# A two-layer hybrid trunk on one core: another pool order, split transposes and a TensorE sum at the start

## The chip, the cores and the metric

The kernel runs on one NeuronCore of one Trainium2 chip. The metric is device time of one execution in microseconds. Three runs of the kernel before gave 1827.31, 1830.92 and 1836.54 us, so the median is 1830.92 us.

## The reference

One step of a two-layer trunk on 640 tokens of width 1024 (512 latent tokens, 128 context tokens), all in float32:

- adaLN modulation: `m = silu(cond) @ w_mod + b_mod`, one vector of 6 x 1024 for each of the two conditions and each layer, `w_mod` being 1024 x 6144 in each layer;
- sub-layer 1: `h = rms(x) * (1 + scale) + shift`, one input projection `h @ w_in`, and three head groups beside each other: a diagonal complex state-space scan in both directions, latent attention with eight heads, and chunked gMLP. Then a norm for each group, one output projection and a gated residual;
- sub-layer 2: the second modulated norm, a gated feed-forward layer with a depthwise convolution of width 3 (`d_ff` 2816), and a gated residual.

For the scan each state needs `a_bar = exp(A * dt)` with `dt = exp(log_dt)`, its powers, and `(a_bar - 1) / A`. These come from `ssm_a_re`, `ssm_a_im` and `ssm_log_dt`. The initial states `state_ssm_re` and `state_ssm_im` enter only where a scan starts.

## The kernel before, in words

Activations are held transposed: `xT` is 128 partitions x 8 x 642, the eight slices (`k`) being the eight blocks of 128 features, with the latent tokens in columns 0 to 511 and the context tokens in 514 to 641. Each product of the large projections is three matmuls on split operands (`mm3`, lines 141 to 143): weights are loaded into a `raw` buffer, ScalarE rounds them to `whi` (L117) and VectorE makes the remainder `wlo` (L118). Token columns are done in two halves.

A planner orders the instructions: it takes them by the order of the program, simulates when their operands and buffers are ready, and writes one fixed stream for each engine. Within its stream an engine executes strictly in order. DMAs are issued from the streams of SP (SPq), ScalarE (ACTq) and GpSimd (POOL), so an issue that waits holds what stands behind it. A buffer can be overwritten only when all its readers are done, and pools that are opened after another was closed on the same side take the same addresses, so that they wait for the former users.

The start of the program, in the order of `run`:

- `consts`, `cond`: the identity matrix, and SiLU of the two conditioning vectors as `sT`.
- `ssm_scalars`: five 64x64 tables (real and imaginary part of A, `log_dt`, two states) are loaded on ACTq (L455, L450), transposed by TensorE into one PSUM bank `ssc`, and copied as one piece into `stab` (L460, L461). From there VectorE alone computes `dt`, sine, cosine, exponentials and powers (`exp_parts`, `sincos`, `complex_mul`; L384 to L436 and L470 to L522). Its last operations write `pw`, `rho`, `sf` and `r8`.
- `params(0)`: rows of small parameters are loaded from GpSimd's queue into a pool `prm0` on the right side, transposed by TensorE (`pa<-rows`), and copied by VectorE into `prm` and `cw` (L189, L198). The pool is closed.
- `load_x`: five tiles of 128 tokens (four `x_sample`, one `x_prompt`) are loaded by SPq into the three `raw` buffers of the pool `wp`, transposed by TensorE (`xin`), and copied to `xT` by ScalarE (L289).
- A pool `pre` on the right side, with eight `raw` buffers for `w_mod`: its addresses are those of `prm0`. `mod_blocks` loads four blocks of 512 columns, each in four loads of 512 KB (L257), multiplies them by `sT` (L261), copies the result (L267, `modev`), transposes it (`modt`) and reduces it (L240 to L247) to the columns of `mod`.
- `begin_layer`: the sum of squares of `xT` for the first half (`norm_stats`), the reciprocal root (`rsqrt`), the broadcast (`bcast`, `nbc`) and the modulated norm (`norm_apply`: `nt` L353, `hh` L357, `hl` L358). The second half follows at the head of `mixers` through `norm`. `norm_stats` squares the eight slices on ScalarE into `nsq` (L331); VectorE adds them to `nacc` (L332); TensorE sums over the partitions with a column of ones (L341, `nst`).

Then `mixers` starts. The pool `ssm` lies on the right side where `pre` lay, and its first use is a memset of `uT` on GpSimd (L870). GpSimd then computes the scan's rotation tables (`Tr`) and the tables of one of the four groups of channels (`q = 3`), while VectorE makes those of `q = 0, 1, 2` (`bb`, `G`, `Q`; `ssm_tables`), with transposes on TensorE (`we`). The tables go to DRAM and are loaded again for the scans (L690 to L696). The pool with `hh` and `hl` lies on the left side where the pool of `ssm_scalars` lay (memsets L1665).

Of the kernel before, what the change touches and what calls it, by code (L numbers as in the profile page):

```python
# [10 lines left out]
F32 = mybir.dt.float32  # L11
F32R = mybir.dt.float32r
I32 = mybir.dt.int32
AF = mybir.ActivationFunctionType
OP = mybir.AluOpType
# [5 lines left out]
KT = 8  # L21
# [13 lines left out]
def bc(ap, shape):  # L35
    return ap.to_broadcast(list(shape))
# [11 lines left out]
class Trunk:  # L48
# [260 lines left out]

    def norm(self, pool, l, which, lo, hi, hh, hl):  # L310

        r = self.norm_stats(pool, lo, hi)

        def rest():
            pb = self.pz("nbc")
            self.bcast(pool, *r, pb)
            self.norm_apply(pool, l, which, lo, hi, hh, hl, pb)

        return rest

    def norm_stats(self, pool, lo, hi):

        nc = self.nc
        n = hi - lo
        acc = pool.tile([128, 322], F32, name=self.uid("nacc"), tag="nacc", bufs=2)
        for k in range(KT):
            if k == 0:
                nc.scalar.activation(acc[:, :n], self.xT[:, k, lo:hi], AF.Square)
            else:
                sq = pool.tile([128, 322], F32, name=self.uid("nsq"), tag="nsq", bufs=2)  # L330
                nc.scalar.activation(sq[:, :n], self.xT[:, k, lo:hi], AF.Square)  # L331
                nc.vector.tensor_tensor(acc[:, :n], acc[:, :n], sq[:, :n], op=OP.add)  # L332
        blocks = []
        for a, b, _ in spans(lo, hi):
            blocks += list(range(a, b - 127, 128))
            if (b - a) % 128:
                blocks.append(b - 128)
        nb = len(blocks)
        ps = self.pz("nst")
        for i, b in enumerate(blocks):  # L340
            nc.tensor.matmul(ps[:, i:i + 1], acc[:, b - lo:b - lo + 128], self.ones[:, 0:1],  # L341
                             start=True, stop=True)
        v = self.smt([128, nb], f"nv{nb}")
        nc.vector.tensor_scalar(v, ps[:, :nb], 1.0 / D, EPS, op0=OP.mult, op1=OP.add)
        return self.rsqrt(v, nb), [b - lo for b in blocks]
# [93 lines left out]
    def ssm_scalars(self):  # L439


        nc, cp, I, V = self.nc, self.cp, self.I, self.nc.vector
        with self.tc.tile_pool(name="ssc", bufs=1) as pool:
            ps = self.pa("ssc")
            for i, nm in enumerate(("ssm_a_re", "ssm_a_im", "ssm_log_dt",
                                    "state_ssm_re", "state_ssm_im")):
                rows = pool.tile([64, 64], F32, name=self.uid("srow"), tag="srow", bufs=5)
                if nm == "ssm_log_dt":
                    col = pool.tile([64, 1], F32, name="sdt")
                    nc.scalar.dma_start(  # L450
                        out=col, in_=I[nm].rearrange("l d (g o) -> (l d g) o", o=1))
                    V.tensor_copy(rows, bc(col, [64, 64]))
                else:
                    src = I[nm] if nm[1] == "s" else I[nm][0]
                    nc.scalar.dma_start(out=rows, in_=src.rearrange("l d g p -> (l d g) p"))  # L455
                self.tr(ps[:64, i * 64:(i + 1) * 64], rows, 64)
            tab = pool.tile([128, 5, 32], F32, name="stab")
            pv = ps[:64, :320].rearrange("p (a h g) -> p a h g", a=20, h=2)
            tv = tab.rearrange("p i (a g) -> p (i a) g", g=8)
            V.tensor_copy(tv[0:64], pv[:, :, 0, :])  # L460
            V.tensor_copy(tv[64:128], pv[:, :, 1, :])  # L461
            are, aim = tab[:, 0, :], tab[:, 1, :]
            self.h0 = cp.tile([128, 2, 32], F32, name="h0")
            V.tensor_copy(self.h0, tab[:, 3:5, :])

            def t(s, sh=(128, 32)):
                return pool.tile(list(sh), F32, name=self.uid(s), tag=s)

            ldt = t("ldt")
            V.tensor_copy(ldt, tab[:, 2, :])  # L470
            dt, _ = self.exp_parts(pool, ldt, 32)
            ax = t("ax")
            V.tensor_tensor(ax, are, dt, op=OP.mult)
            th = t("th", (128, 8, 32))
            V.tensor_tensor(th[:, 0], aim, dt, op=OP.mult)
            for j in range(1, 8):
                V.tensor_scalar(th[:, j], th[:, 0], float(1 << (j + 2)), None, op0=OP.mult)
            ea, em = self.exp_parts(pool, ax, 32)
            sn, cm = self.sincos(pool, th.rearrange("p a b -> p (a b)"), 256)
            snv = sn.rearrange("p (a b) -> p a b", a=8)  # L480
            cmv = cm.rearrange("p (a b) -> p a b", a=8)
            self.rho = cp.tile([128, 7, 2, 32], F32, name="rho")
            V.tensor_scalar(self.rho[:, :, 0, :], cmv[:, 1:8], 1.0, None, op0=OP.add)
            V.tensor_copy(self.rho[:, :, 1, :], snv[:, 1:8])
            self.pw = cp.tile([128, 9, 3, 32], F32, name="pw")
            pw = self.pw
            V.memset(pw[:, 0, 0, :], 1.0)
            V.memset(pw[:, 0, 1, :], 0.0)
            x = t("x")
            V.tensor_tensor(x, ea, cmv[:, 0], op=OP.mult)  # L490
            V.tensor_tensor(pw[:, 1, 0, :], x, ea, op=OP.add)
            V.tensor_tensor(pw[:, 1, 1, :], ea, snv[:, 0], op=OP.mult)
            nre = t("nre")
            V.tensor_tensor(nre, x, em, op=OP.add)
            nim = pw[:, 1, 1, :]
            den, d2 = t("den"), t("d2")
            V.tensor_tensor(den, are, are, op=OP.mult)
            V.tensor_tensor(d2, aim, aim, op=OP.mult)
            V.tensor_tensor(den, den, d2, op=OP.add)
            V.reciprocal(den, den)  # L500
            self.f = cp.tile([128, 2, 32], F32, name="sf")
            y1, y2 = t("y1"), t("y2")
            V.tensor_tensor(y1, nre, are, op=OP.mult)
            V.tensor_tensor(y2, nim, aim, op=OP.mult)
            V.tensor_tensor(y1, y1, y2, op=OP.add)
            V.tensor_tensor(self.f[:, 0], y1, den, op=OP.mult)
            V.tensor_tensor(y1, nim, are, op=OP.mult)
            V.tensor_tensor(y2, nre, aim, op=OP.mult)
            V.tensor_tensor(y1, y1, y2, op=OP.subtract)
            V.tensor_tensor(self.f[:, 1], y1, den, op=OP.mult)  # L510
            for k in (1, 2, 4):
                sh = [128, k, 32]
                tm = [t(f"cm{i}{k}", sh) for i in range(2)]
                b_re = bc(pw[:, k:k + 1, 0, :], sh)
                b_im = bc(pw[:, k:k + 1, 1, :], sh)
                self.complex_mul(V, pw[:, k + 1:2 * k + 1, 0, :], pw[:, k + 1:2 * k + 1, 1, :],
                                 pw[:, 1:k + 1, 0, :], pw[:, 1:k + 1, 1, :], b_re, b_im, tm)
            V.tensor_scalar(pw[:, :, 2, :], pw[:, :, 1, :], -1.0, None, op0=OP.mult)
            self.r8 = cp.tile([128, 32], F32, name="r8")
            V.tensor_tensor(self.r8, ea, ea, op=OP.mult)  # L520
            V.tensor_tensor(self.r8, self.r8, self.r8, op=OP.mult)
            V.tensor_tensor(self.r8, self.r8, self.r8, op=OP.mult)  # L522
        self.WEd, self.Qd, self.Td, self.Wd = (
            [[self.dp.tile(sh, F32, name=f"{nm}{l}{q}") for q in range(4)] for l in range(DEPTH)]
            for nm, sh in (("WEd", [128, 2, 2, 2, 128]), ("Qd", [128, 2, 2, 2, 128]),
                           ("Td", [128, 2, 2, 2, NS]), ("Wd", [8, 16, 4, 128])))
        self.Ud = [self.dp.tile([256, 8, NC], F32, name=f"Ud{l}") for l in range(DEPTH)]
        self.Yd = [self.dp.tile([16, 128, NC], F32, name=f"Yd{l}") for l in range(DEPTH)]
# [1077 lines left out]
    def run(self):  # L1606
        nc, tc = self.nc, self.tc
        with self.banks(True):
            self.consts()
            self.cond()  # L1610
            self.ssm_scalars()
            self.params(0)
            self.load_x()
            self.late_consts()
            with tc.tile_pool(name="pre", bufs=1, side="right") as pre:
                mix = self.begin_layer(0, self.mod_blocks(0, (2, 0, 3, 1), pre))
        for l in range(DEPTH):
            sa, sb = self.sides
# [49 lines left out]
    def begin_layer(self, l, modulate=None):  # L1668
# [7 lines left out]
        if modulate:  # L1676
            for _ in range(8):
                next(modulate)
            r = self.norm_stats(N, 0, 320)
            for _ in range(2):  # L1680
                next(modulate, None)
            pb = self.pb("nbc")[:, 0]
# [73 lines left out]
```

## Time and profile before

| what | value |
|---|---|
| median of three runs | 1830.92 us (1827.31 to 1836.54) |
| the profiled execution | 1831.83 us, span 1830.0 us |
| PE busy | 1708.6 us, 93% of the span |
| PEld busy | 1499.7 us, 82% |
| DVE busy | 1158.5 us, 63% |
| ACT busy | 681.7 us, 37% |
| POOL busy | 311.4 us, 17% |
| DMA, mean | 100 GB/s, 182.44 MB |
| chain that ended last | PE 75%, DVE 10%, DMA 8%, ACT 4% |

The span runs from the first to the last instruction; the profiled execution's own time is 1.8 us longer than it. Busy shares are means over the whole span: the first 300 us and the rest have different limits, and the table does not tell them apart. The rows further below do.

### The profile page before, as it was taken

The page shows a single profiled execution, that of the slowest core. Times are in us where ns is not written, and L with a number is a line of the kernel's source. Part 1 is how long each engine was busy: PE and PEld are TensorE (multiplying, and loading weights), DVE is VectorE, ACT ScalarE, POOL GpSimd, SP SyncE. Part 2 cuts the span into 40 slices and gives each one's busy share as a digit, 9 for nine tenths or more (in the row PEclk, how much of TensorE's full clock was granted, in tenths as well). Part 3 has the DMA queues.
Part 4 walks back from the last instruction along what each step waited for, and adds up shares of the span by engine and source line. Part 5 has one row for each costly group of instructions (what it writes and reads, how often), then busy time and mean ns, then how long its engine had stood idle before and what let it go on. Part 6 is the DMA issues. An engine that isn't in the chain of part 4 may idle for free.

```text
span 1830.0 us, 28203 instructions
## 1 busy us (share of the span) xinstructions
PE 1708.6 (93%) x10864; PEld 1499.7 (82%) x10864; DVE 1158.5 (63%) x2421; ACT 681.7 (37%) x1210; POOL 311.4 (17%) x738
## 2 busy tenths in 40 slices
PE   6869789998999999999999888999989999999998
PEld 2668644478889999999999785445989999999998
DVE  6887875667664546456566668475786464555554
ACT  4334444433442424224244355353344232332241
POOL 2886200000195060540000210000000000000000
PEclk8989799999999999999999888999989999999999
DMA  9265453301453523223122633430222131221221
GB/s 297 70 177 152 113 166 122 105 24 47 129 160 111 152 55 117 76 81 110 47 78 79 169 87 121 157 127 1 70 70 93 35 104 47 92 89 39 81 82 58
DMA packets 192998, 182.44 MB, mean 100 GB/s; under 512 B 33438, under 2 KB 153052, under 8 KB 192864
## 3 DMA queue, kind: packets, MB, share of 16 engines
q1 hardware_dynamic: 170160, 154.33, 27.5%
q0 software_dynamic: 8272, 23.87, 4.4%
q10 hardware_dynamic: 14432, 2.44, 0.7%
q8 instruction: 86, 1.41, 0.3%
q14 instruction: 48, 0.39, 0.1%
HBM read 161.94 MB, written 18.64 MB: 99 GB/s over the span
## 4 chain that ended last, share of the span: by engine, by line
PE 75%; DVE 10%; DMA 8%; ACT 4%; issue 2%; POOL 1%; ACTq 1%; DVEq 0%; POOLq 0%
PE up L141 11%; PE up L143 11%; PE up L142 10%; PE dn L142 5%; PE dn L143 5%; PE dn L141 5%; PE mod L261 3%; DMA raw<-w_mod 3%; PE o L1287 3%; PE wo L141 1%; PE wo L143 1%; PE wo L142 1%; DVE wlo L118 1%; DMA raw<-ffn_w_up 1%; PE s L1267 1%
## 5 line engine op out<-in xcount | busy, mean ns | idle before, releaser
L141 PE MATMUL up<-hh,whi 128*128 128x322 f32 x1408 | 436.8, 315 | 9.8 <-ACT hh L357 8.9
L142 PE MATMUL up<-hl,whi 128*128 128x322 f32 x1408 | 439.2, 313 | 1.8 <-DVE hl L358 1.8
L143 PE MATMUL up<-hh,wlo 128*128 128x322 f32 x1408 | 439.8, 314 | 0.0
L141 PEld LDWEIGHTS up<-hh,whi 128*128 128x128 f32 x1408 | 266.1, 190 | 21.8 <-issue 10.8
L142 PEld LDWEIGHTS up<-hl,whi 128*128 128x128 f32 x1408 | 268.3, 191 | 2.7 <-DVE hl L358 2.7
L143 PEld LDWEIGHTS up<-hh,wlo 128*128 128x128 f32 x1408 | 267.3, 190 | 1.0 <-issue 1.0
L118 DVE TENSOR_TENSOR wlo<-raw,whi 128x1024 fp32r<-128x1024 f32 (+1 forms) x116 | 147.4, 1272 | 155.2 <-ACT whi L117 146.5
L142 PE MATMUL dn<-glo,dh 128*128 128x322 f32 (+1 forms) x704 | 217.7, 311 | 0.0
L143 PE MATMUL dn<-gh,dl 128*128 128x322 f32 (+1 forms) x704 | 217.4, 310 | 0.0
L141 PE MATMUL dn<-gh,dh 128*128 128x322 f32 (+1 forms) x704 | 208.9, 310 | 2.3 <-DVE xT L1501 1.5
L1501 DVE SCALAR_TENSOR_TENSOR xT<-dn,mod,xT 128x320 f32<-128x320 f32 (+2 forms) x288 | 112.1, 435 | 128.2 <-PE dn L143 128.1
L117 ACT CAST whi<-raw 128x1024 fp32r<-128x1024 f32 (+1 forms) x116 | 120.6, 1041 | 157.1 <-PE up L142 63.8
L1532 ACT ACTIVATE cv<-up,prm,cw 128x321 f32<-128x321 f32 x88 | 54.1, 619 | 259.0 <-PE up L143 255.0
L143 PEld LDWEIGHTS dn<-gh,dl 128*128 128x128 f32 x704 | 132.9, 189 | 0.0
L141 PEld LDWEIGHTS dn<-gh,dh 128*128 128x128 f32 x704 | 130.4, 189 | 2.8 <-DVE xT L1501 1.8
L142 PEld LDWEIGHTS dn<-glo,dh 128*128 128x128 f32 x704 | 132.7, 188 | 0.0
L261 PE MATMUL mod<-raw,sT 128*32 128x512 f32 x384 | 89.7, 642 | 21.7 <-DMA raw<-w_mod 19.8
L1533 DVE SCALAR_TENSOR_TENSOR cv<-up,cw,cv 128x320 f32<-128x320 f32 x88 | 48.3, 549 | 74.3 <-ACT cv L1532 74.1
L118 DVE TENSOR_TENSOR dl<-raw,dh 128x1024 fp32r<-128x1024 f32 x44 | 53.9, 1224 | 38.3 <-ACT dh L117 38.2
L1250 DVE TENSOR_REDUCE nml<-mx 128x1 f32<-128x640 f32 x64 | 51.1, 819 | 28.3 <-PE mx L1248 28.2
L117 ACT CAST dh<-raw 128x1024 fp32r<-128x1024 f32 x44 | 46.1, 1048 | 50.7 <-DMA raw<-ffn_w_down 44.5
L141 PE MATMUL wo<-yh,whi 128*128 128x322 f32 (+1 forms) x192 | 60.0, 318 | 1.7 <-ACT yh L117 0.9
(472 smaller groups left out, 3367.4 us busy)
## 6 DMA issues: line engine op xcount, KB each, us to landing
raw<-w_mod SPq DMA_DIRECT2D x96, 512.0 KB, 4.3
raw<-ffn_w_up SPq DMA_DIRECT2D x88, 512.0 KB, 3.9
raw<-ffn_w_down SPq DMA_DIRECT2D x44, 512.0 KB, 3.4
raw<-w_in SPq DMA_DIRECT2D x10, 512.0 KB, 5.0
we<-WEd POOLq DMA_DIRECT2D x8, 512.0 KB, 4.4
qt<-Qd POOLq DMA_DIRECT2D x8, 512.0 KB, 5.0
raw<-w_out SPq DMA_DIRECT2D x16, 256.0 KB, 4.8
raw<-w_out SPq DMA_DIRECT2D x8, 512.0 KB, 3.4
```

What stands on the lines that cost most here:

```text
L117: self.nc.scalar.copy(hi, raw)
L118: self.nc.vector.tensor_tensor(lo, raw, hi.bitcast(F32), op=OP.subtract)
L141: mm(ps, wh, xh, start=start, stop=False)
L142: mm(ps, wh, xl, start=False, stop=False)
L143: mm(ps, wl, xh, start=False, stop=stop)
L261: nc.tensor.matmul(ps[c:c + 32, :], self.sT[:, k, :], rv[:, j, :], start=k < 4, stop=k >= 4)
L1250: V.tensor_reduce(nm[:, tt:tt + 1], pb[:, :, :320], axis=AX.XY, op=OP.max, negate=True)
L1267: mm(ps, kh[i][:, kc_], qh[i], start=True, stop=False)
L1287: mm(pb[i * 64:(i + 1) * 64, 0], Vt[:, kt, 2 * p + i], Ps[i][kt], start=kt == 0, stop=kt == 4)
L1501: self.nc.vector.scalar_tensor_tensor(self.xT[:, m, a:b], po[:, a - lo:b - lo], self.modcol(l, gi, m, c), self.xT[:, m, a:b], op0=OP.mult, ...
L1532: A.activation(z[:, 0:321], po[:, 0:321], AF.Identity, bias=b, scale=c1)
L1533: V.scalar_tensor_tensor(z[:, 1:321], po[:, 0:320], c0, z[:, 1:321], op0=OP.mult, op1=OP.add)
```

## The change

Four edits, all of which act ahead of the first matmul on the modulated activations of layer 0:

1. The pool `pre` is opened ahead of `cond`, `ssm_scalars`, `params(0)` and `load_x`, so that its addresses are no longer those of `prm0`.
2. `ssm_scalars` transposes `log_dt` and the two parts of A first, into one bank, and copies them to `stab`. The two states are transposed into another bank at the end of the function and copied straight to `h0`.
3. `norm_stats` gets an argument. Where it is 0 (the first norm of layer 0, both halves) no `nacc` is made: TensorE multiplies each `nsq` by the column of ones and accumulates over the eight slices in one bank.
4. That bank comes from the pool `PA` (two banks at this stage) and not from `PS`.

```diff
-        r = self.norm_stats(pool, lo, hi)
+        r = self.norm_stats(pool, lo, hi, l + which)
...
-    def norm_stats(self, pool, lo, hi):
+    def norm_stats(self, pool, lo, hi, l=1):
...
+        ps = None if l else self.pa("nst")
+        acc = pool.tile([128, 322], F32, name=self.uid("nacc"), tag="nacc", bufs=2) if l else None
+        for k in range(KT):
+            if k == 0 and l:
+                nc.scalar.activation(acc[:, :n], self.xT[:, k, lo:hi], AF.Square)
+                continue
+            sq = pool.tile([128, 322], F32, name=self.uid("nsq"), tag="nsq", bufs=2)
+            nc.scalar.activation(sq[:, :n], self.xT[:, k, lo:hi], AF.Square)
+            if l:
+                nc.vector.tensor_tensor(acc[:, :n], acc[:, :n], sq[:, :n], op=OP.add)
+                continue
+            for i, b in enumerate(blocks):
+                nc.tensor.matmul(ps[:, i:i + 1], sq[:, b - lo:b - lo + 128], self.ones[:, 0:1],
+                                 start=k == 0 and i == 0, stop=k == KT - 1 and i == nb - 1)
...
+            tab = pool.tile([128, 3, 32], F32, name="stab")
+            rows_of(("ssm_log_dt", "ssm_a_re", "ssm_a_im"), tab)
...
+            self.h0 = cp.tile([128, 2, 32], F32, name="h0")
+            rows_of(("state_ssm_re", "state_ssm_im"), self.h0)
...
-            self.cond()
-            self.ssm_scalars()
-            self.params(0)
-            self.load_x()
-            self.late_consts()
             with tc.tile_pool(name="pre", bufs=1, side="right") as pre:
+                self.cond()
+                self.ssm_scalars()
+                self.params(0)
+                self.load_x()
+                self.late_consts()
                 mix = self.begin_layer(0, self.mod_blocks(0, (2, 0, 3, 1), pre))
...
-            r = self.norm_stats(N, 0, 320)
+            r = self.norm_stats(N, 0, 320, l)
```

`rows_of(names, tile)` is the former loop of loads and transposes over the given names, followed by the two copies of the bank to the two halves of the partitions of `tile`.

## Rows read from the trace of the kernel before

**Rows 1.** The page: busy tenths of the span in 40 equal slices.
```profile
PE   6869789998999999999999888999989999999998
...
POOL 2886200000195060540000210000000000000000
```

**Rows 2.** Windows to 55 us: busy us and count of each engine, clock, DMA share, GB/s.
```profile
0.00:10.00 10.00, 3.92 (x16) 3.02 (x17) 0.43 (x4) 2.48 (x3) 7.21 (x20) 1.00 0.68 195
10.00:20.00 10.00, 7.30 (x35) 6.16 (x33) 4.38 (x26) 4.73 (x7) 4.45 (x13) 1.00 0.91 247
20.00:35.00 15.00, 9.69 (x32) 1.67 (x32) 13.51 (x52) 8.60 (x18) 0.00 (x0) 0.66 1.01 341
35.00:50.00 15.00, 11.17 (x46) 3.11 (x46) 14.49 (x81) 3.08 (x5) 0.00 (x0) 0.89 1.00 354
50.00:55.00 5.00, 2.35 (x14) 1.33 (x15) 5.00 (x25) 2.02 (x6) 1.96 (x14) 1.00 0.16 41
```

**Rows 3.** Timeline of GpSimd: start us, us, what, idle before and its releaser.
```profile
50.75 0.12 POOL L1665 MEMSET hh<- 128x16 f32 x1 [35.26 <-issue]
...
53.16 0.13 POOL L870 MEMSET uT<- 128x16 f32 x1 [2.23 <-PE mod L261]
...
151.63 0.61 POOL L690 DMA_DIRECT2D we<-WEd  x1
```

**Rows 4.** Windows from 53 us to the scans' first load.
```profile
53.00:70.00 17.00, 15.09 (x97) 14.43 (x96) 12.84 (x37) 7.39 (x18) 16.79 (x62) 0.90 0.10 11
70.00:110.00 40.00, 32.97 (x229) 28.91 (x228) 37.06 (x88) 16.60 (x47) 38.20 (x104) 0.96 0.45 118
110.00:151.60 41.60, 30.86 (x264) 26.28 (x265) 33.59 (x75) 15.03 (x41) 32.73 (x71) 0.79 0.67 183
```

**Rows 5.** Timeline of VectorE: the scan constants' first copy, the parameter copy, the last powers.
```profile
11.89 0.32 DVE L460 COPY stab<-ssc 64x160 f32<-64x160 f32 x1 [5.39 <-PE ssc L147]
...
19.01 0.27 DVE L189 COPY prm<-pa 128x109 f32<-128x109 f32 x1 [3.45 <-PE pa L147]
...
51.33 0.31 DVE L518 TENSOR_SCALAR pw<-pw 128x288 f32<-128x288 f32 x1
```

**Rows 6.** Timeline of TensorE: transposes of tables, x tiles and parameters, and the last modulation matmuls.
```profile
6.55 0.31 PE L147 MATMUL ssc<-ident,srow 64*64 64x64 f32 x1 [1.97 <-DVE srow L452]
...
15.32 3.56 PE L147 MATMUL xin<-ident,raw 128*128 128x128 f32 x16 [1.57 <-DMA raw<-x_sample]
18.72 0.38 PE L147 MATMUL pa<-ident,rows 109*128 109x109 f32 x3
...
52.03 1.05 PE L261 MATMUL mod<-raw,sT 128*32 128x512 f32 x4
```

**Rows 7.** Timeline of SP's DMA issues to 55 us.
```profile
2.00 7.87 SPq L284 DMA_DIRECT2D raw<-x_sample  x4
...
13.78 3.88 SPq L134 DMA_DIRECT2D raw<-w_in  x2
...
19.65 12.97 SPq L257 DMA_DIRECT2D raw<-w_mod  x10
...
35.87 3.75 SPq L257 DMA_DIRECT2D raw<-w_mod  x4
```

**Rows 8.** Groups on VectorE, 10 to 55 us: count, busy us, mean ns, idle before.
```profile
L332 DVE TENSOR_TENSOR nacc<-nacc,nsq 128x320 f32<-128x320 f32 (+1 forms) x14 | 6.8, 486 | 1.5 <-ACT nsq L331 1.5
L118 DVE TENSOR_TENSOR wtl<-raw,wth 128x576 fp32r<-128x576 f32 x4 | 3.0, 747 | 0.0
...
L118 DVE TENSOR_TENSOR wlo<-raw,whi 128x1024 fp32r<-128x1024 f32 x2 | 2.4, 1216 | 0.0
```

**Rows 9.** Chain of waits, 15 to 60 us: one addition's step (start us, us).
```profile
33.63 0.41 DVE nacc L332
```

**Rows 10.** TensorE: the partition sums (timeline), and its waits from 100 to 150 us.
```profile
36.54 0.83 PE L341 MATMUL nst<-ones,nacc 128*128 128x1 f32 x6 [1.78 <-DVE modred L240]
...
PE we L147 <- DVE G L95: 11.8, 2, 8.8
```

More of the change, by code (lines that the diff above doesn't have):

```diff
@@ L319, in norm @@
         return rest
-    def norm_stats(self, pool, lo, hi):
+    def norm_stats(self, pool, lo, hi, l=1):
         nc = self.nc
         n = hi - lo
[L325 to L332, printed above, removed]
         blocks = []
@@ L338, in norm_stats @@
         nb = len(blocks)
[L339 to L342, printed above, removed]
+        ps = None if l else self.pa("nst")
[12 more added lines that the diff above has]
+                                 start=k == 0 and i == 0, stop=k == KT - 1 and i == nb - 1)
+        if l:
+            ps = self.pz("nst")
+            for i, b in enumerate(blocks):
+                nc.tensor.matmul(ps[:, i:i + 1], acc[:, b - lo:b - lo + 128], self.ones[:, 0:1],
+                                 start=True, stop=True)
         v = self.smt([128, nb], f"nv{nb}")
@@ L443, in ssm_scalars @@
         with self.tc.tile_pool(name="ssc", bufs=1) as pool:
[L444 to L464, printed above, removed]
+            def rows_of(nms, tile):
+                ps = self.pa("ssc")
+                n = len(nms)
+                for i, nm in enumerate(nms):
+                    rows = pool.tile([64, 64], F32, name=self.uid("srow"), tag="srow", bufs=5)
+                    if nm == "ssm_log_dt":
+                        col = pool.tile([64, 1], F32, name="sdt")
+                        nc.scalar.dma_start(
+                            out=col, in_=I[nm].rearrange("l d (g o) -> (l d g) o", o=1))
+                        V.tensor_copy(rows, bc(col, [64, 64]))
+                    else:
+                        src = I[nm] if nm[1] == "s" else I[nm][0]
+                        nc.scalar.dma_start(out=rows, in_=src.rearrange("l d g p -> (l d g) p"))
+                    self.tr(ps[:64, i * 64:(i + 1) * 64], rows, 64)
+                pv = ps[:64, :n * 64].rearrange("p (a h g) -> p a h g", a=4 * n, h=2)
+                tv = tile.rearrange("p i (a g) -> p (i a) g", g=8)
+                V.tensor_copy(tv[0:64], pv[:, :, 0, :])
+                V.tensor_copy(tv[64:128], pv[:, :, 1, :])
@@ L466, in t @@
+            tab = pool.tile([128, 3, 32], F32, name="stab")
+            rows_of(("ssm_log_dt", "ssm_a_re", "ssm_a_im"), tab)
+            are, aim = tab[:, 1, :], tab[:, 2, :]
             def t(s, sh=(128, 32)):
@@ L469, in ssm_scalars @@
             ldt = t("ldt")
-            V.tensor_copy(ldt, tab[:, 2, :])
+            V.tensor_copy(ldt, tab[:, 0, :])
             dt, _ = self.exp_parts(pool, ldt, 32)
```

## Prediction

> **What bounds the kernel now.** I read the forty slices first: PE is at eight or nine tenths nearly everywhere but in the first slices, and POOL works almost only in the first fifth of the span [rows 1]. All edits act ahead of 55 us, so the question is what limits that stretch and whether a shorter one ends the kernel earlier.
>
> I then cut the start into windows [rows 2]. Up to 20 us no engine is full: VectorE is busy 0.43 us of the first ten and 4.38 us of the next. From 20 to 55 us VectorE is busy 33.0 of 35 us, and the DMA engines are at 1.00 to 1.01 until 50 us, moving 341 to 354 GB/s. TensorE is busy only 23.2 of the last 35 us. So two limits lie beside each other: VectorE's stream, and the bytes of `w_mod`.
>
> The view of GpSimd shows what the two release [rows 3]. Its first real work in the mixer stands behind the memset of `hh` at 50.75 us, which needs the pool of `ssm_scalars` back (VectorE's last powers come at 51.33 us [rows 5]), and behind the memset of `uT` at 53.16 us, which the trace puts down to the last modulation matmuls; these start at 52.03 us [rows 6], and they free the last buffers of `pre`. From there to the scans' load of `we` at 151.63 us GpSimd is busy 16.79 + 38.20 + 32.73 = 87.7 of 98.6 us, 89%, VectorE 85% [rows 4]. Hence what is gained at 53 us should be passed on nearly whole: there is no slack at either engine to swallow it. I measure the change by the time at which GpSimd gets past that memset.
>
> **The change part by part.**
>
> *Squares on TensorE.* VectorE loses 14 additions of 486 ns busy [rows 8]. They overlap with their neighbours, and in the chain one takes 0.41 us [rows 9]: 14 x 0.41 = 5.7 us. VectorE is full there, so I take 5.7 (at least 0, if another limit comes first; at most the 6.8 us of the group).
>
> TensorE gets, for each half, eight slices x three blocks in place of three blocks. Three blocks are six instructions (two passes each) and take 0.83 us [rows 10]. So 12 instructions become 96: 84 more at 0.83 / 6 = 0.138 us, 11.6 us. That cover exists: TensorE is busy 34.4 of the 55 us [rows 2], 20.6 us idle. I count 0 for it. If the order of the streams puts the sums of the first half (5.8 us) where a modulation matmul would run, it costs up to 5.8 us; second-half sums are needed only after the first half's norm. The squares no longer wait for VectorE to free a buffer but for TensorE, whose stream waits for DMA; the modulation matmuls and the PSUM copies stand behind such a sum.
>
> *Scan constants apart from the states.* The copy to `stab` now needs three tables. The last of these was transposed at 6.55 + 0.31 = 6.86 us [rows 6], against 11.89 us for the copy [rows 5]: 5.0 us of head start. But VectorE then stops at the copy of `prm` until 19.01 us (3.45 us of waiting now). What the head start yields is the work that the planner now puts ahead of that copy: between 0 and 5.0 us, and I take the middle, 2.5. The two states cost two more narrow copies and save one to `h0`; I call that 0 (within 0.3 us either way, the first two copies being 0.32 us apiece).
>
> *`pre` opened first.* The first load of `w_mod` stood at 19.65 us, just after the transposes of the parameter rows at 18.72 us [rows 6, 7], whose addresses it reused. Now eight loads (4.19 MB) may go out as soon as SP's stream comes to them. By bytes, the first 20 us moved 1.95 + 2.47 = 4.42 MB; at the 341 GB/s of the next window it could have been 6.82 MB, so 2.4 MB or 7.0 us are free [rows 2]. By the DMA share of the same rows only 0.32 x 10 + 0.09 x 10 = 4.1 us are. In addition SP's stream had five loads of `w_in` ahead of the last `w_mod` issues; the first two alone are 1.05 MB, 3.1 us at 341 GB/s [rows 7]. If they fall behind, the last modulation matmul comes between 4.1 and 10.1 us earlier. I take 10, next to the upper end, since the order of the program puts `w_mod` ahead of `w_in` and only the missing buffers had reversed it.
>
> With `w_in` later, its splits leave VectorE's stream ahead of the last powers: these are 3.0 + 2.4 = 5.4 us [rows 8]. Between 0 and 5.4; I take 2.0, because some of them still fit.
>
> One page of the Trainium skill speaks against this part. DMA: Bandwidth & Descriptors, section "Issuing engines are not separate DMA queues", says that transfers from any issuing engine end on the same 16 DMA engines and interleave, so an early start buys only what these engines had free. By that the share, not the bytes, is the measure, and the sum below would have 4.1 + 3.1 = 7.2 us where it has 10. The rows on the first 20 us, a share of 0.68 and 0.91 at 195 and 247 GB/s, do not decide: the share is high while the rate is low.
>
> *Sum.* VectorE's side: 5.7 + 2.5 + 2.0 = 10.2 us. DMA side: 10. The later of the two sets GpSimd's start, so 10 us: from 53.2 to about 43 us. What is late next is TensorE (below) and then again VectorE, which from 70 to 110 us is busy 37.06 of 40 us [rows 4]. Against the profiled execution's own time that is 1831.83 - 10 = 1821.8 us; that execution lies 0.9 us above the median of the runs, so for a median I say 1821 us.
>
> **The rivals.**
>
> *The x tiles fall behind `w_mod` on SP's stream.* The fourth x load waits for a `raw` buffer of `wp`; eight `w_mod` loads may now stand ahead of it and of `x_prompt`, 4.19 MB, 12.3 us at 341 GB/s. TensorE's transposes of parameters stand behind those of the x tiles (15.32 to 18.72 us [rows 6]), and VectorE's stream behind `prm` at 19.01 us. For it: both streams are in order. Against it: the planner has to put the parameters behind the late x tiles again. If half of the 12.3 us comes through, VectorE's gain shrinks from 10.2 to about 4 us: 1827 us.
>
> *TensorE becomes the limit.* Its 34.4 us of work and 11.6 us of new sums start at 3.3 us and have to wait for the first x tiles: in the first 20 us it idles 20 - 11.2 = 8.8 us. 34.4 + 5.8 (first half) + 8.8 = 49 us is then the earliest time for the last modulation matmul, 4 us better than now: 1827 us. For it: those matmuls are in one stream with the sums. Against it: part of the idle time is filled by the early `w_mod`.
>
> *The order after 55 us comes out worse.* The planner writes all streams anew. TensorE stood still at `we` transposes that waited for VectorE's `G`: two waits of 11.8 us together between 100 and 150 us, the longest 8.8 [rows 10], with runnable projection matmuls behind. There are six such groups (three tables, two directions). With VectorE's splits of `w_in` pushed later, between its tables, four more of them may be hit: 4 x 5.9 = 23.6 us, less 10, is 13.6 us slower, 1844 us. Two such waits more (11.8 us) turn the sign. For it: VectorE has only 15% of slack there. Against it: the tables themselves can start earlier.
>
> *The change doesn't do what it says* (SP's stream still has `w_mod` behind x and `w_in`): only VectorE's 5.7 + 2.5 counts, and the modulation holds GpSimd at 53 us: 1830 us.
>
> **How the numbers follow.** Forecast 0.54, x tiles behind 0.14, TensorE 0.12, no effect 0.06, worse order 0.14. The forecast alone spans 1815 to 1828 us (the DMA side at 4.1 us, or VectorE's terms at their upper ends, 6.8 + 5.0 + 5.4 = 17 us). Cases of both signs leave the range at 1812 to 1836 us: below lie the upper ends of all terms together, above most of the worse order. About 0.5% is what a measurement of this kernel can tell from no change, 9.2 us, so "faster" means below 1821.8 us. The forecast lies at that edge: some 0.80 of its chance on the faster side if the bounds of the DMA side are lopsided upward as argued, nothing of the others: 0.43. Slower by over 0.5%: most of the worse order and little else, 0.12. The rest, 0.45, is the same.
>
> **What would show it.** Right: the first `w_mod` issue before 10 us; `stab` copied near 7 us; no `nacc` until layer 0's second norm; VectorE's last `pw` near 41 us; the memset of `uT` near 43 us; the scans' load of `we` some 10 us ahead of 151.63. Wrong: the copy of `prm` after 22 us; PE busy without gaps from 15 us to the last modulation matmul; waits of `we` for `G` above 12 us between 90 and 150 us; or an earlier `uT` with the scans' load where it was, which would mean that the gain is lost between the two.

## Result: slower by 1.4%

Four runs of the changed kernel gave 1851.81 to 1864.02 us, median 1861.35; the kernel before on the same chip had a median of 1833.72. The ratio is 1.0139, 95% interval 1.0105 to 1.0173. The forecast was 1821, with a range of 1812 to 1836 and 0.12 on "slower".

The edits do what they say: `w_mod` goes out early, the first copy to `stab` is 96 columns wide in place of 160, and `nacc` is first written at 458.6 us. The windows of the changed kernel (columns as in [rows 2]) show early bytes and a new limit:

```profile
0.00:10.00 10.00, 3.30 (x14) 2.47 (x15) 1.59 (x13) 2.48 (x3) 7.21 (x20) 1.00 0.68 208
10.00:20.00 10.00, 8.72 (x41) 4.71 (x39) 6.97 (x45) 3.37 (x5) 4.51 (x13) 1.00 1.04 348
20.00:35.00 15.00, 12.96 (x56) 7.75 (x58) 11.71 (x65) 3.21 (x6) 0.00 (x0) 0.59 1.09 358
35.00:50.00 15.00, 15.00 (x56) 8.10 (x54) 7.48 (x42) 5.21 (x12) 0.17 (x2) 0.50 0.50 164
50.00:55.00 5.00, 5.00 (x21) 3.50 (x17) 1.91 (x3) 2.83 (x5) 0.00 (x0) 0.50 0.23 57
55.00:70.00 15.00, 15.00 (x59) 9.96 (x59) 8.23 (x20) 5.53 (x11) 5.16 (x33) 0.50 0.39 98
```

From 10 to 20 us 348 GB/s move where it was 247. VectorE, full before, is half idle from 35 us on. TensorE shows no idle time from 35 to 70 us and waits for nothing there, at a granted clock of 0.50, the lower of its two levels (1.2 GHz); before it had 0.89 and 1.00 up to 55 us [rows 2]. The timelines of SP, VectorE (the copy of the scan constants, the last powers) and GpSimd, one fence for each, answer to [rows 7], [rows 5] and [rows 3]:

```profile
4.12 2.09 SPq L257 DMA_DIRECT2D raw<-w_mod  x2
```
```profile
8.80 0.25 DVE L469 COPY stab<-ssc 64x96 f32<-64x96 f32 x1 [5.57 <-PE ssc L147]
...
44.46 0.32 DVE L527 TENSOR_SCALAR pw<-pw 128x288 f32<-128x288 f32 x1
```
```profile
64.64 0.12 POOL L881 MEMSET uT<- 128x16 f32 x1 [27.52 <-DMA raw<-w_in]
...
165.73 0.57 POOL L701 DMA_DIRECT2D we<-WEd  x1 [4.11 <-PE e L727]
```

The first `w_mod` issue comes at 4.12 us (before 19.65), `stab` 3.1 us and the last powers 6.9 us earlier. But `uT`, which I had at 43, comes at 64.64: 11.5 us late in place of 10 early. TensorE's timeline shows why (answers to [rows 6, 10]):

```profile
36.37 1.44 PE L344 MATMUL nst<-ones,nsq 128*128 128x1 f32 x6
37.74 1.92 PE L261 MATMUL mod<-raw,sT 128*32 128x512 f32 x4
39.59 1.44 PE L344 MATMUL nst<-ones,nsq 128*128 128x1 f32 x6
40.96 1.92 PE L261 MATMUL mod<-raw,sT 128*32 128x512 f32 x4
...
62.62 1.08 PE L261 MATMUL mod<-raw,sT 128*32 128x512 f32 x4
```

Sums and modulation matmuls alternate in one stream. Six instructions of sums take 1.44 us (0.83 before) and four of the modulation 1.92 us (1.05). The last modulation matmuls start at 62.62 us in place of 52.03.

Then a second loss follows, far behind the edits. The four scan groups last from the first `e` matmul to the last `y` matmul. Windows over just that stretch, first before, then after:

```profile
147.60:210.80 63.20, 54.89 (x413) 48.97 (x413) 50.76 (x119) 27.00 (x60) 28.04 (x81) 0.89 0.47 133
```
```profile
161.50:243.10 81.60, 68.76 (x453) 62.04 (x453) 51.81 (x137) 32.93 (x70) 29.11 (x90) 0.81 0.37 108
```

They took 63.2 us and now take 81.6, with 40 more matmuls inside, VectorE busy as long as before (50.8, 51.8 us) but idle for 29.8 us in place of 12.4. VectorE runs the scan itself. The waits that ended its idle time up to the first `y<-hq` matmul (us, times, longest), before and after:

```profile
DVE hq L761 <- DMA Td<-Tr: 2.2, 1, 2.2
DVE wlo L118 <- ACT whi L117: 2.0, 1, 2.0
```
```profile
DVE wlo L118 <- ACT whi L117: 7.9, 2, 6.2
DVE krg L1139 <- DMA Wd<-we: 4.6, 1, 4.6
```

In the new stream, operations of the attention branch that wait for ScalarE or a DMA stand ahead of the scan's steps. VectorE's timeline between two steps of the first scan group, the products `m` and `hq`, which is computed from them, before and after:

```profile
161.47 0.94 DVE L755 TENSOR_TENSOR m<-H,T 128x656 f32<-128x656 f32 x1
...
173.31 0.32 DVE L761 TENSOR_TENSOR hq<-m 64x164 f32<-64x164 f32 x1 [2.19 <-DMA Td<-Tr]
...
177.19 0.96 DVE L118 TENSOR_TENSOR wlo<-raw,whi 128x768 fp32r<-128x768 f32 x1 [1.14 <-ACT whi L117]
```
```profile
175.67 0.84 DVE L766 TENSOR_TENSOR m<-H,T 128x656 f32<-128x656 f32 x1
...
190.90 0.96 DVE L118 TENSOR_TENSOR wlo<-raw,whi 128x768 fp32r<-128x768 f32 x1 [6.21 <-ACT whi L117]
...
194.36 0.31 DVE L772 TENSOR_TENSOR hq<-m 64x164 f32<-64x164 f32 x1
```

The `wlo` of 768 columns belongs to the attention's query weights (`w_uq`). It stood behind `hq` and now stands ahead of it, with a wait of 6.2 us; from `m` to `hq` 11.8 us become 18.7. The delay grows from 13.9 us at the first `e` to 32.3 at the last `y`, and is 31.1 us at the end of the span: nothing is added later.

### The profile page after: what moved, and what is told of

It reads as the page before. It is cut to its first block, busy times and chain, and to the rows that moved or that the text cites. A ratio compares the mean times of both kernels' runs of the same rounds, so it can differ in the third digit from the quotient of the medians.

```text
span 1861.1 us, 28368 instructions
## 1 busy us (share of the span) xinstructions
PE 1739.4 (93%) x10948; PEld 1522.4 (82%) x10948; DVE 1154.5 (62%) x2408; ACT 681.0 (37%) x1210; POOL 309.0 (17%) x738
## 5 line engine op out<-in xcount | busy, mean ns | idle before, releaser
L261 PE MATMUL mod<-raw,sT 128*32 128x512 f32 x384 | 95.6, 687 | 13.6 <-DMA raw<-w_mod 13.6
L1544 DVE SCALAR_TENSOR_TENSOR cv<-up,cw,cv 128x320 f32<-128x320 f32 x88 | 48.3, 550 | 68.6 <-ACT cv L1543 68.4
```

Source lines behind the costliest of these rows:

```text
L261: nc.tensor.matmul(ps[c:c + 32, :], self.sT[:, k, :], rv[:, j, :], start=k < 4, stop=k >= 4)
L1544: V.scalar_tensor_tensor(z[:, 1:321], po[:, 0:320], c0, z[:, 1:321], op0=OP.mult, op1=OP.add)
```

## Experiments

One view of every profiled execution, starts in us: the memset of `uT`, GpSimd's first `bb` (the first operation of its tables that needs loaded data), the first `e` matmul, and the end of the last `y`. "Own" is the planner's own order. "Old" is the issue order of the kernel before for every instruction from the memset of `uT` on. The ratio is to the kernel before on the same chip. A milestone is read from one execution, a ratio from many. The profiled execution of the kernel before took 1831.83 us, while that kernel's medians beside the experiments are 1835.20 to 1838.63 us, so the two need not agree to within some 7 us (0.4%).

| kernel | order | uT | bb | e | last y | ratio (95%) |
|---|---|---|---|---|---|---|
| before | own | 53.2 | 59.8 | 147.6 | 210.8 | 1 |
| after | own | 64.6 | 69.8 | 161.5 | 243.1 | 1.0139 (1.0105 to 1.0173) |
| pool | own | 52.7 | 61.0 | 150.4 | 226.9 | 1.0000 (0.9977 to 1.0023) |
| split | own | 55.1 | 60.1 | 152.1 | 222.5 | 1.0033 (1.0013 to 1.0054) |
| sums | own | 63.6 | 68.6 | 149.1 | 235.1 | 1.0089 (1.0059 to 1.0119) |
| pool_split | own | 51.7 | 59.4 | 148.2 | 218.7 | 1.0026 (0.9999 to 1.0053) |
| swap_before | after's | 50.3 | 62.5 | 152.2 | 233.4 | 1.0060 (1.0033 to 1.0087) |
| pin_after | old | 59.6 | 66.5 | 156.5 | 220.5 | 1.0017 (0.9988 to 1.0046) |
| pin_sums | old | 56.5 | 62.3 | 150.4 | 216.6 | 1.0042 (1.0016 to 1.0069) |
| pin_pool_split | old | 45.4 | 60.7 | 149.4 | 212.3 | 0.9995 (0.9974 to 1.0016) |
| pin_pool_split_sp | old | 46.3 | 61.6 | 151.7 | 217.9 | 1.0033 (1.0015 to 1.0051) |
| pin_sp | old | 50.0 | 62.6 | 153.2 | 217.9 | 1.0038 (1.0019 to 1.0057) |
| pin_wide | old | 50.7 | 62.5 | 150.0 | 213.0 | 1.0013 (0.9995 to 1.0031) |
| wide | own | 55.4 | 62.2 | 142.8 | 234.6 | 1.0094 (1.0064 to 1.0124) |
| pin_pool_split_pb | old | 45.9 | 54.4 | 145.0 | 210.6 | 0.9974 (0.9957 to 0.9992) |
| pin_before_pb | old | 56.1 | 62.6 | 150.0 | 218.1 | 1.0022 (1.0002 to 1.0042) |
| pin_wide_pb | old | 49.8 | 58.0 | 148.1 | 211.0 | 1.0013 (0.9993 to 1.0034) |

**The parts alone.** Each kernel takes whole parts of the change and nothing else (in short):

```diff
+ pool:  with tc.tile_pool(name="pre", ...) as pre:  ahead of self.cond()
+ split: rows_of(("ssm_log_dt", "ssm_a_re", "ssm_a_im"), tab) ... rows_of((states), self.h0)
+ sums:  norm_stats(pool, lo, hi, l), nst accumulated over the eight slices
+ pool_split: the first two together
```

> Only the pool pre opened first. Theory S (TensorE's sums of squares are the cause of the late start: 96 instructions in order among the modulation matmuls, at a granted clock of 0.50): without them the modulation ends earlier than before, memset of uT at 47 to 51 us (53.2 before, 64.6 after), time 1820 to 1832 us. Rival P (the early w_mod loads hold ScalarE's stream, whose issue of dcol waited 7 us for a w_mod load): uT at 56 us or later, 1840 us or more. Rival O (any new order of the streams costs some 15 us in the four scan groups, which took 59 us before and 78 us after): uT early but the four groups at 70 us or more, 1835 to 1845 us.

> Only the scan constants apart from the states. Theory S: VectorE starts them at 8 to 9 us in place of 11.9, the w_mod loads still start near 19.6 us, uT at 51 to 53 us, time 1826 to 1834 us. Rival P: the same, since w_mod is not early. Rival O: the four scan groups at 70 us or more in place of 59, 1840 to 1850 us.

> Only TensorE's sums of squares. Theory S: TensorE busy without gaps at a clock of 0.50 from about 27 us until the last modulation matmul at 60 us or later, uT at 60 to 66 us, time 1842 to 1856 us. Rival P: uT within 2 us of 53, time 1825 to 1835 us. Rival O: like P at uT, with the groups at 70 us or more, 1845 us.

> The pool pre opened first and the scan constants apart, squares added on VectorE as before. Theory S: the gain that was forecast for the whole change, uT at 42 to 47 us, time 1818 to 1828 us. Rival P: uT at 56 us or later, 1840 us or more. Rival O: uT early, the four scan groups at 70 us or more, 1835 to 1845 us.

Of the theories named there, S (the sums stretch the head at the low clock) holds for the sums, but not for the rest: in the other three kernels `uT` came 1.7 to 4.7 us later than S allowed, and pool_split's gain did not come. P (early `w_mod` loads hold ScalarE behind an issue of `dcol`) falls: ScalarE is held like that in the changed kernel, 7.0 us at 28.63 us, but TensorE waits for its squares only once, 1.8 us, and the early pool alone loses nothing. O (any new order costs in the scan groups) is borne out in direction: from the first `e` to the last `y` the four kernels take 7 to 23 us longer than the kernel before. The sums are the only part that makes the head late by more than 2 us (`uT` +10.4 us), and the costliest. The early pool alone costs nothing, and its `uT` comes 0.4 us earlier, not 10. All four have a later last `y` than the kernel before, by 8 to 24 us, even pool_split, whose first `e` is only 0.6 us late. But a late last `y` is not yet time lost: in pool it is 16.1 us late and the time is the same. From the last `y` to the end the profiled executions of the table take 1614 to 1628 us, the kernel before 1619.

**The order by itself.** Issue-order edges, which add no wait, chain every engine's instructions from the memset of `uT` on. The head stays with the planner, which plans it anew for each kernel.

```diff
+        trunk(tc, I, O, dbg)
+        for seq in ORDER.values():      # one list per engine: the order of the other kernel
+            for a, b in zip(seq[:-1], seq[1:]):
+                tc.add_manual_dep(ins[b], ins[a].name, NoSync, reason="order")
```

> The whole change, but from the memset of uT on every engine issues its instructions in the order that the kernel before has; only the head is new. Theory S+O (two causes: the sums delay the head by about 11 us, and the new order of the streams behind it costs some 20 us): uT at 60 to 66 us, from the first to the last matmul of the four scan groups 60 to 68 us as before (63 us; 82 us in the changed kernel), time 8 to 15 us above the kernel before. Rival H (the order only follows from the late head, and is the best for it): 25 us above it or more.

> The kernel before in all its computation, but from the memset of uT on every engine issues in the order of the changed kernel. Theory S+O: uT within 2 us of 53 us, the four scan groups 75 to 85 us, time 12 to 22 us above the kernel before. Rival H: with the early head the order costs nothing, within 4 us of the kernel before.

With the old order the whole change is at 1.0017; with the new order the kernel before, none of the edits in it, is at 1.0060. Both have the scan groups that S+O named, and both times, some 3 and 11 us above the kernel before, lie below its ranges. The kernel before in the new order has scan groups (window over them) like those of the changed kernel, with the same wait:

```profile
152.20:233.40 81.20, 68.66 (x452) 61.72 (x452) 51.63 (x136) 33.09 (x70) 29.33 (x92) 0.81 0.37 107
```
```profile
181.22 0.96 DVE L118 TENSOR_TENSOR wlo<-raw,whi 128x768 fp32r<-128x768 f32 x1 [6.22 <-ACT whi L117]
...
184.68 0.31 DVE L761 TENSOR_TENSOR hq<-m 64x164 f32<-64x164 f32 x1
```

That the order is only the consequence of a late head (H, as quoted up to here) falls with this: `uT` is 2.9 us early here, and early too in pool and pool_split, while a rise within 4 us was H's forecast and 11 us were measured. So the order alone accounts for the longer scan stage: 81.2 us here, 81.6 after, against 63.2 before and 64.0 with the changed kernel in the old order.

> Only TensorE's sums, with the order of the kernel before from the memset of uT on. Theory S+O: uT at 61 to 65 us, groups 60 to 68 us, time 8 to 13 us above the kernel before (the sums with a free order were 17 above). Rival H: 17 us above or more. Rival N (the late head is absorbed on the way, since the sums' kernel had its first scan matmul only 1.5 us late): within 4 us of the kernel before.

> The pool and the split transposes, squares on VectorE, with the order of the kernel before from the memset of uT on. Theory S+O: uT at 50 to 52 us, groups 60 to 66 us, time 1 to 5 us below the kernel before (with a free order it was 4 above). Rival H: the same 4 us above as with a free order, or more.

In the old order the sums alone make `uT` 3.3 us late, the whole change 6.4 us, and the time says 1.0042 and 1.0017. The time does not follow `uT`, but that a late head is absorbed (N) isn't shown: 0.42% is 7.7 us, outside N's 4 us, and the two intervals overlap. For an early head it is shown. Without the sums `uT` comes at 45.4 us, 7.7 us early, and the last modulation matmuls start at 44.26 in place of 52.03. Yet the first `e` is 1.8 us late and the time the same. GpSimd's timeline in pin_pool_split shows a hole behind its rotations, ScalarE's queue the issues that fill it:

```profile
53.26 0.31 POOL L93 TENSOR_TENSOR Tr<-Tr,rho 128x64 f32<-128x64 f32 x1
60.72 0.24 POOL L91 TENSOR_TENSOR bb<-B,sf 128x32 f32<-128x32 f32 x1 [7.15 <-DMA B<-ssm_b_re]
```
```profile
53.98 0.62 ACTq L550 DMA_DIRECT2D B<-ssm_b_re  x1
55.06 0.61 ACTq L550 DMA_DIRECT2D B<-ssm_b_im  x1
56.02 0.60 ACTq L550 DMA_DIRECT2D B<-ssm_b_re  x1
...
58.59 0.60 ACTq L550 DMA_DIRECT2D B<-ssm_b_re  x1
```

By the names of the buffers, the issue at 53.98 is for VectorE's second table; it has to wait until VectorE has read the only `B` buffer of its first (last read at 53.77 us). GpSimd's own loads, which wait for nothing of VectorE's, follow from 56.02 on; the last one that its first `bb` needs is issued at 58.59 and lands 2.1 us later, at 60.7. Before, the same queue started at 52.23 us, and `bb` ran without a wait straight behind the rotations:

```profile
59.75 0.24 POOL L91 TENSOR_TENSOR bb<-B,sf 128x32 f32<-128x32 f32 x1
```

**Taking the wait away.** First by another queue:

```diff
+        ld = nc.sync if l == 0 else nc.scalar
-                    nc.scalar.dma_start(out=B[...    # also Cr, dcol
+                    ld.dma_start(out=B[...
```

> The early pool and the apart scan constants, in the old order of issue, with the loads of B, Cr and dcol of layer 0 issued by SyncE in place of ScalarE. Without that move the uT memset ran at 45.42 (before: 53.16), yet the first e matmul at 149.4, last y at 212.3, ratio 0.9995. Theory Q (ScalarE's issues hold the gain): the first B issue stood behind ScalarE's hh work at 53.98, GpSimd waited 7.1 us for B and ScalarE 11.49 us behind 18 issues of 0.64 us each; with the loads on an idle queue GpSimd starts the first bb some 7 us earlier, first e comes at 141 to 144, last y at 204 to 207, ratio 0.994 to 0.998. Rival G (the wait only moves: another engine's row between 55 and 150 us, TensorE's tr or ScalarE's own copies, sets the first e): uT about 45, first e at 147 to 150, last y at 210 to 214, ratio 0.999 to 1.001.

> The kernel before in its own order, with the loads of B, Cr and dcol of layer 0 issued by SyncE: the control for the run above. Theory Q: before, GpSimd did not wait for B (its uT memset was at 53.16, the first B issue at 52.23), so the move alone frees ScalarE, which GpSimd did not wait for: first e at 146 to 148.5, ratio 0.998 to 1.001. Rival R (the 24 issues on ScalarE cost time in themselves, by the hh halves behind them): first e at 142 to 145, ratio 0.995 to 0.998, and then a lower time in the run above says nothing on the head.

Q (ScalarE's issues hold the gain) fell. Its rival G and both forecasts for the control missed too: both kernels are 0.3 to 0.4% slower. The wait went along with the loads. SP's queue in pin_pool_split_sp, and GpSimd's timeline:

```profile
SPq L551 <- DVE G L93: 2.7, 1, 2.7
```
```profile
61.58 0.24 POOL L91 TENSOR_TENSOR bb<-B,sf 128x32 f32<-128x32 f32 x1 [7.22 <-DMA B<-ssm_b_re]
```

Another queue with the same buffer does not remove the wait. So the second attempt gives GpSimd's table a buffer of its own and lets GpSimd, idle from 15 to 43 us, issue its eight loads, which are left out of the chained order:

```diff
+        if l == 0 and E is nc.gpsimd:
+            B = self.tb0.tile([128, 2, 2, 2, 16], F32, name=self.uid("B"), tag="B3")
+            ld = nc.gpsimd
```

> The early pool and the apart scan constants in the old order of issue, with the eight loads of B for the fourth table (GpSimd's) issued by GpSimd itself in the head, into a buffer of their own. Without that: uT memset 45.42, GpSimd's first bb at 60.7 after a wait of 7.1 us for B, first e at 149.4, last y 212.3, ratio 0.9995. Theory B (the first table's single B buffer holds the loads behind it, and GpSimd's bb sets the first e some 88 us later: 59.75 to 147.6 before, 60.7 to 149.4, 62.5 to 150.0): bb at 53 to 55, no wait for B, first e at 141 to 144, last y at 204 to 207, ratio 0.994 to 0.998. Rival V (another engine sets the first e; the 88 us are a coincidence): bb at 53 to 55, first e still 147 to 151, ratio 0.998 to 1.002.

> The kernel before, in its own order, with the same early loads of B: the control. GpSimd did not wait for B there (bb at 59.75 straight after its rotations). Theory B: bb at 58.5 to 60, first e at 146 to 148.5, ratio 0.998 to 1.001. Rival V' (the eight issues taken off ScalarE, 5 us, are a gain by themselves): first e at 142 to 145, ratio 0.995 to 0.998; the run above then says less.

> The whole change in the old order, with sums 128 columns wide and the early loads of B. Without the loads: uT 50.71, GpSimd's first bb at 62.5 after 4.4 us of wait, first e at 150.0, last y 213.0, ratio 1.0013. Theory B: bb at 57.5 to 59, first e at 145 to 147, last y at 208 to 210, ratio 0.997 to 1.000. Rival V: bb earlier, first e at 149 to 151, ratio 1.000 to 1.003.

GpSimd's timeline in pin_pool_split_pb:

```profile
12.75 0.65 POOL L556 DMA_DIRECT2D B<-ssm_b_re  x1
...
45.89 0.12 POOL L881 MEMSET uT<- 128x16 f32 x1 [2.26 <-DMA raw<-w_in]
...
54.43 0.48 POOL L91 TENSOR_TENSOR bb<-B,sf 128x32 f32<-128x32 f32 x1
```

`bb` moves from 60.7 to 54.4, the first `e` from 149.4 to 145.0, the last `y` from 212.3 to 210.6: 6.3 us become 4.4 and then 1.7. The ratio, 0.9974, has its interval wholly under 1 and is the lowest of all kernels here; that it gains on pin_pool_split's 0.9995 isn't shown, as the two intervals overlap. Theory B (the single buffer holds GpSimd's loads, and its `bb` sets the first `e`) named the wait rightly, and its ratio came in; it overrated what passes: `e` was expected at 141 to 144, the last `y` at 204 to 207. The control did not gain; outside every forecast for it, its head came 2.9 us later (`uT` 56.1) and it is 0.2% slower. With that late head it says little of what the loads give alone. In pin_wide_pb `bb` and the milestones behind came 1.9 to 4.5 us earlier, and the ratio stayed at 1.0013, against Theory B's 0.997 to 1.000; 2 us are 0.1%, which these intervals don't resolve.

**The clock.** Each sum 128 columns wide, a matrix of ones in place of the column:

```diff
-                nc.tensor.matmul(ps[:, i:i + 1], sq[:, b - lo:b - lo + 128], self.ones[:, 0:1],
+                nc.tensor.matmul(ps[:, i * 128:i * 128 + 128], sq[:, b - lo:b - lo + 128], self.ones,
```

> The whole change in the old order of issue, with each of the 84 products of the sums 128 columns wide (a matrix of ones) in place of one column; the result is read from one column. Rows to go by: six of one column took 0.73 to 0.83 us at the high clock and 1.44 at the low one; six of 128 columns (nbc) 0.94 and 1.63. With one column the granted clock was 0.50 from 35 to 55 us and uT came at 59.59. Theory K (the one-column products are what leaves the clock low): granted clock 0.85 to 1.00 from 35 to 55 us, mod x4 at 1.05 us, uT at 49 to 55, ratio 0.997 to 1.001. Rival L (the clock is low for another reason, the waits in between or the early start; more columns only add 84 x 0.032 = 2.7 us): granted clock 0.50 to 0.60, uT at 60 to 64, ratio 1.001 to 1.005.

> The whole change in the planner's own order, with sums 128 columns wide. With one column and this order: uT 64.64, first e 161.5, scan groups 82 us, last y 243.1, ratio 1.0139; in the old order, wide: uT 50.71, last y 213.0, ratio 1.0013. Theory H (the planner's new order costs whatever the clock; it does not know the clock and moves instructions for the added ones): uT at 50 to 57, scan groups 70 to 82 us, ratio 1.004 to 1.010. Rival N (the bad order only hurts because the head is late): scan groups 62 to 66 us, ratio 0.999 to 1.003.

Windows of pin_after (one column), of pin_wide, and pin_wide's TensorE timeline:

```profile
35.00:50.00 15.00, 15.00 (x62) 9.96 (x60) 9.33 (x33) 6.04 (x11) 0.17 (x2) 0.50 0.64 204
```
```profile
35.00:50.00 15.00, 13.74 (x92) 8.33 (x90) 11.96 (x44) 7.73 (x14) 0.17 (x2) 1.00 0.71 227
50.00:55.00 5.00, 3.54 (x23) 2.53 (x20) 3.80 (x18) 2.75 (x5) 4.24 (x21) 1.00 0.46 110
```
```profile
30.10 1.05 PE L261 MATMUL mod<-raw,sT 128*32 128x512 f32 x4
31.09 0.94 PE L344 MATMUL nst<-ones,nsq 128*128 128x128 f32 x6
31.95 1.05 PE L261 MATMUL mod<-raw,sT 128*32 128x512 f32 x4
```

Theory K (the one-column products leave the clock low) holds for the clock and for `uT`: 128 times the columns, and six instructions of sums take 0.94 us in place of 1.44, four of the modulation 1.05 in place of 1.92, as the clock is at its upper level (1.00) from 20 to 70 us. `uT` comes 8.9 us earlier than in pin_after. The two heads were planned separately and their streams part after some 28 us, so not all of this need be the clock. In time it is not seen (1.0013, just above K's 1.001, and 1.0017, intervals that overlap). In the planner's own order (wide) the first `e` is at 142.8, the earliest of all kernels, and it is still 0.94% slower, its scan groups being the longest, 91.8 us:

```profile
142.80:234.60 91.80, 71.75 (x457) 64.14 (x457) 55.75 (x137) 34.31 (x73) 33.09 (x109) 0.81 0.36 106
```
```profile
DVE wlo L118 <- ACT whi L117: 13.0, 3, 6.4
DVE krg L1140 <- DMA Wd<-we: 6.9, 1, 6.9
```

The waits are VectorE's, up to the first `y<-hq`. Of the theories of this run (the letters H and N mean others than above), H, that the planner's own order costs even at the upper clock, holds in its ratio but not in its upper bound for the scan groups, 82 us; N, that only a late head makes the order bad, fell.

## Why the prediction was wrong, step by step

1. **DMA side, 10 us: of the right size in the old order only.** `w_mod` went out at 4.12 us. Without the sums and in the old order `uT` came 6.9 to 7.7 us earlier in three kernels, within my span of 4.1 to 10.1. In the planner's own order the same two edits moved it by 1.5 us (pool_split), and swap_before, with no edit in the head, has 2.9 us by the planning alone. By the share of [rows 2] the sum was 7.2 us. The Trainium skill (DMA: Bandwidth & Descriptors, "Issuing engines are not separate DMA queues") says that loads from all issuing engines run on the same 16 DMA engines and interleave; from that I had drawn that the share counts. The 6.9 to 7.7 us agree better with it than with my bytes, but the scatter of the heads is as large as the difference, and VectorE's side, not shown apart, may have a part in it.

2. **VectorE's side, 10.2 us: not tested as a sum.** The additions are gone, and `pw` is 6.9 us earlier. VectorE stopped being the limit, so what it was worth doesn't show. Two readings were wrong. The memset of `hh` ran at 50.75 us, ahead of the last powers at 51.33 [rows 3, 5], so it didn't wait for these. And if the later of two sides sets the time, a DMA side of at most 10.1 us allows no forecast below about 1821 us; the lower end of 1815 used VectorE's 17 us alone.

3. **TensorE's 84 more instructions, counted as 0: failed, and it set the head.** The rival "TensorE becomes the limit" had the mechanism with 0.12, and its sign came in part (TensorE busy without gaps up to the last modulation matmul, here from 26 us). But it priced the work as it ran in the rows before, at clocks of 0.66 to 1.00: 49 us for the last modulation matmul, against 62.62. Between pin_pool_split and pin_wide, which differ by wide sums alone, `uT` is 5.3 us later; between pin_pool_split and pin_after, with one-column sums, 14.2. So the sums cost some 5 us on the path by their number and some 9 by the clock, give or take the scatter of the heads of some 3 us, where I had 0 and at most 5.8. Without the early pool they cost 3.3 us in the old order (pin_sums) and 10.4 in the planner's. I read the idle time of [rows 2] as cover; but the sums stand in the stream ahead of the modulation matmuls, and 0.83 us for six [rows 10] was taken in a stretch at 0.89, while the window before it in the same rows, at 0.66, already warned that the clock here is not a constant.

4. **"Passed on nearly whole, no slack at either engine": failed.** I looked at GpSimd's busy share behind `uT` [rows 4] and not at what its second step waits for. Its first `bb` needs a load that stands behind VectorE's release of a buffer; that wait was just hidden before and took all 7.7 us when `uT` moved. With it gone (pin_pool_split_pb) 2.6 us reach the first `e` and 0.2 us the last `y`. The time is 0.26% lower, 4.8 us, more than these milestones explain.

5. **"The order after 55 us comes out worse", 0.14 at 1844: the main loss, in the wrong place.** I had it at the `we` transposes between 100 and 150 us. From 100 to 160 us the changed kernel's waits of that kind were shorter, 3.2 us where [rows 10] has 11.8. The order cost 18 us in the scan groups. Exchanging it, with no edit of the computation, is worth 1.0139 to 1.0017 in the changed kernel, 1.0094 to 1.0013 with wide sums, and 1 to 1.0060 in the kernel before; for sums and pool_split the intervals of both orders overlap, and pool's own order costs no time. A rewritten order has no price in the profile of before; all six kernels here that have an order of their own, and differ from before in a few edits ahead of 55 us, have a later last `y`.

So of the 1.39% the order of the streams behind the edits makes the larger part, some 1.2%, and what is left with the late head in pin_after, 0.17%, is not clear of zero.

What stays open: why the planner puts attention work ahead of the scans each time; why pool makes good its late last `y`; and the scatter of 0.2 to 0.4% among the kernels in the old order, whose heads were still planned anew (pin_sp, pin_before_pb). I would not read a cause into any one of these.

## To carry to other kernels

Where a planner writes the streams, pin the old order behind an edit before judging the edit: here up to 1.2% was decided some 100 us behind the last changed instruction. "No slack behind this point" is shown by following what the next few operations wait for, queue and buffer included, not by a busy share. A count of new matmuls is priced at both clock levels, and counted as hidden only if they stand behind the critical ones in their stream.

## What the runs showed of the hardware

A busy TensorE can sit at the low clock. In the changed kernel the profile, which models the ends of matmuls, has it busy 15.00 of 15 us from 35 to 50 and again from 55 to 70 us at a granted clock of 0.50, while one-column sums alternated with modulation matmuls; with 128 columns a stream of the same work had 1.00 from 10 to 70 us, in three kernels (pin_wide, wide, pin_wide_pb). One column does not hold the clock down for good, as two windows of pin_sums show:

```profile
20.00:35.00 15.00, 15.00 (x67) 10.65 (x68) 13.85 (x60) 6.12 (x11) 0.00 (x0) 0.50 1.06 352
35.00:50.00 15.00, 15.00 (x98) 8.23 (x92) 13.60 (x78) 7.38 (x18) 0.17 (x2) 0.96 1.04 368
```

The Trainium skill (TensorE: Matmul & The Clock Gate, "HAM oscillation — how this bites in real kernels") puts such falls down to DMA waits between groups of matmuls and advises, for a thin M, to reorder the loop or to pad M. The waits do not fit here, as the trace shows none for TensorE from 35 to 70 us. A padding did help, though of the moving columns and in a stream without such waits, which is not the page's case.

An issue that waits for a buffer holds what stands behind it on its queue. By the names of the buffers, GpSimd's load waited for nothing itself but stood behind one that did, and the 7.2 us of GpSimd's wait came with the loads to SP's queue (7.15 us on ScalarE's).
